# A third column pair by seven block products in the second layer's first FFN, with the key/value side work spread over fewer blocks

## The chip, the cores and the metric

The kernel runs on one core of a Trainium2 chip, as one launch. The metric is device time in microseconds (us), the median of several runs. TensorE is PE in the profile, its weight loads PEld, VectorE is DVE, ScalarE is ACT, GpSimd is POOL and SyncE is SP.

## The reference, cut to what matters

Two layers work on 256 tokens of width 1024, in float32. Each layer is a half step of SwiGLU, an attention, and a second half step of SwiGLU. After the first layer, keys and values for the second layer's attention are derived once.

```python
def _swiglu(x, w_in, w_out):
    a, b = jnp.split(x @ w_in, 2, axis=-1)
    return (jax.nn.silu(a) * b) @ w_out

for layer in range(DEPTH):
    h = h + 0.5 * _swiglu(_rmsnorm(h, ffn1_norm[layer]), ffn1_w_in[layer], ffn1_w_out[layer])
    hn = _rmsnorm(h, mix_norm[layer])
    ...
    h = h + 0.5 * _swiglu(_rmsnorm(h, ffn2_norm[layer]), ffn2_w_in[layer], ffn2_w_out[layer])
    if layer == N_A_LAYERS - 1:
        kvs = _nsa_shared_kv(h, kv_norm, nsa_w_kv, nsa_k_norm, cmp_pos_k, cmp_pos_v, ...)
```

`w_in` is 1024 x 5632 and `w_out` is 2816 x 1024. `_nsa_shared_kv` projects `h` to keys and values, compresses two of the six groups by a small hidden layer (`_compress`), normalizes and rotates the keys.

## The kernel before, in words

**Precision.** Every weight tile of 128 x 1024 (a *unit*) arrives by DMA as float32 and is split in two fp32r tiles: ScalarE writes the high part `wh` (L222), VectorE the rest `wl` (L226). Each product is then three matmuls (`mm3`, L290 to L292): high by high, high by low, low by high. The class `Weights` walks one long list of units in order: `pump` splits the next one, `take` hands it to TensorE, `done` gives its buffers back. There are six buffers each for `wh` and `wl`, and five for arriving tiles. An engine takes its instructions strictly in the order in which they were written to its queue; a scheduler makes that order before the run.

**Ordinary blocks.** The input projection of an FFN is cut into 11 blocks of 256 columns of `a` and the matching 256 of `b`. A block takes four units and 48 matmuls of 512 columns, in four pieces (`proj_block`): two units by the first 128 tokens, the same two by the other 128, then the other two units in the same way. `gate` (L648 to L659) makes silu(a)*b of a token half, and `gtrans` (L661 to L672) transposes a block's gates on TensorE (`gTp`) and splits them.

**Pairs.** Two neighbouring blocks can be done together by Strassen's scheme (Winograd's form): seven products p1 to p7 of block sums, in place of eight. A product is two units and 12 matmuls. The sums of the activations are made once (`sums_of_h`), the sums of weights per pair. In the other three FFNs the weight sums come partly by DMA; in this one, `f11` (second layer, first FFN), VectorE makes them: L228 (`keep` plus the joined tile), L234 (`keep` plus a raw tile), L221 (a raw tile plus a held one), two of 128 x 1024 for each of the four kinds of step, eight in a pair. A pair also has two sums on product banks (`x`, L759).

**The order of a pair** is a string in `FAST`. A digit is a product, `c` is an output chunk (`chunk`: one unit of `w_out`, 12 matmuls into the four `o` banks), `m` transposes one block's gates, `s` runs one piece of side work. `FAST["f11"]` has ordinary blocks 0 to 6, then the pairs (7, 8) and (9, 10), with eight chunks in each.

**Side work.** Beside the ordinary blocks of `f11` run 15 pieces of the key/value work (the list `side` at the end of `kv_phase`): compressed keys are transposed (`c_trans`, `xtp`), GpSimd adds positions (`c_blocks`, L1224), `c_split` splits the result, `c_hidden` 0 to 3 (two units of `cmp` each, 16 matmuls of 256 columns into the bank `hid`), `k_trans` 0 and 1 (`kTp`), `c_out` (transposes `hidT`), `c_out2` (`co`), `c_key` with `c_val_t` (`vcT`), and `c_key_t` (`kcT`). `hid` is finished by a copy on ScalarE (L1254), a sum on VectorE (L1255) and a silu on ScalarE (L1256) before `hidT`. In the loop over ordinary blocks, a piece of side work was run after pieces 1 and 3 of each block; the fifteenth by the `s` of pair (7, 8). `CMP_J = 4` placed the `cmp` units in the list of units.

Of the kernel before, what the change touches and what calls it, by code (L numbers as in the profile page):

```python
# [16 lines left out]
P = 128  # L17
# [2 lines left out]
FF = 2816  # L20
NB = FF // 256
J1 = 6
CMP_J = 4
LOW = 100


FAST = {"f10": (0,1,2,(3,"cccm1ctc5ct367xx24"),(5,"mc1mct5ct3c67xx24"),(7,"mc1mct5ct3c67xx24"),(9,"mc1mct5t36724")),
# [3 lines left out]


# [45 lines left out]
class Sum:  # L78


    def __init__(self, key, load=None, join=None, last=False):
        self.key, self.load, self.join, self.last = key, load, join, last
        self.more = ()


class Unit:


    def __init__(self, ap, key=None, of=None, hold=None, held=None):
        self.ap, self.key, self.of, self.hold, self.held = ap, key, of, hold, held  # L90
        self.more = ()


class Weights:


    def __init__(self, tc, pool, units, raws, bufs):
        self.tc, self.nc, self.pool, self.units = tc, tc.nc, pool, units
        self.raws, self.bufs = raws, bufs
        self.raw, self.hi, self.lo = {}, {}, {}  # L100
        self.on_pool = ()
        self.keep, self.kept, self.missed, self.waiting, self.held = None, {}, 0, [], {}
        self.limit, self.turn, self.pin = len(units), 0, False
        self.jobs, self.jobs_from = [], 0
        self.spans, self.extra = [], None
        self.nr = self.nl = self.ns = self.nt = self.nd = 0
# [94 lines left out]
    def pump(self, slack=1, low=LOW):  # L201

        u = self.ns
        if u >= (self.limit if slack else len(self.units)) or not self.room(u, slack):
            return False
        x = self.units[u]
        if self.keep is None and not isinstance(x, bass.AP) and x.key or self.apart(u) and self.extra is None:
            return False
        while self.nl <= u:
            self.load()  # L210
        nc = self.nc
        n = x.shape[-1] if isinstance(x, bass.AP) else 1024
        hi, lo = self.hi[u], self.lo[u] = self.pair_of(u)
        if not isinstance(x, Sum):
            raw = self.raw.pop(u)
        else:
            raw = self.kept.pop(x.key) if x.last else self.kept[x.key]
        prio = self.tc.cur_priority
        self.tc.cur_priority = prio + low
        if isinstance(x, Unit) and x.held:  # L220
            nc.vector.tensor_tensor(raw, raw, self.held.pop(x.held), op=OP.add)  # L221
        i = nc.scalar.activation(hi[:, 0:n], raw[:, 0:n], AF.Copy)  # L222
        if self.pin:
            self.tc.keep_in_program_order(i)
        e = nc.gpsimd if u in self.on_pool else nc.vector
        e.tensor_tensor(lo[:, 0:n], raw[:, 0:n], hi[:, 0:n].bitcast(F32), op=OP.subtract)  # L226
        if isinstance(x, Sum) and x.join is not None:
            nc.vector.tensor_tensor(raw, raw, self.raw.pop(u), op=OP.add)  # L228
        if isinstance(x, Unit) and x.hold:
            self.held[x.hold] = raw  # L230
        if isinstance(x, Unit) and x.key:
            y = self.kept[x.of or x.key]
            t = self.tile_of(x.key) if x.of else y
            nc.vector.tensor_tensor(t, y, raw, op=OP.add)  # L234
        for op in () if isinstance(x, bass.AP) else x.more:
            if self.keep is None:
                self.waiting.append(op)
            else:
                self.sum_op(*op)
        self.tc.cur_priority = prio  # L240
        self.ns += 1
        self.load()
        if self.jobs and u >= self.jobs_from:
            self.jobs.pop(0)()
        return True
# [13 lines left out]
def build(tc, ctx, a, out):  # L259
    nc = tc.nc  # L260
# [34 lines left out]
    units = []  # L295
# [54 lines left out]
    def fast(l):  # L350

        b = lambda j, k: [a[l[:2] + "i" + l[2]][4 * j + 2 * k + i] for i in range(2)]
        v, r = [], range(2)
        outs = [a[l[:2] + "o" + l[2]][i] for i in chunk_order(l)]
        pairs = [e[0] for e in FAST[l] if isinstance(e, tuple)]

        def also(d, op):
            if isinstance(v[d], bass.AP):
                v[d] = Unit(v[d])
            v[d].more += (op,)  # L360

        for e in FAST[l]:
            if not isinstance(e, tuple):
                v += b(e, 0) + b(e, 1)
                continue
            j, pat, *n = e
            z = pairs.index(j)
            b11, b21, b12, b22 = b(j, 0), b(j, 1), b(j + 1, 0), b(j + 1, 1)
            key = [(j, "t", i) for i in r]
            at = stored.get((l, j))  # L370
            third = lambda z, i: (pairs[z], 2, i)
            kept = lambda last=False: [Sum(key[i], last=last) for i in r]
            plus = [(third(z, i), b22[i], True) for i in r] if at is None else []
            own = l != "f11"
            ahead = []
            if own and z == 0 and at is None:
                for i in r:
                    also(i - 2, (third(0, i), b12[i], False))
            if own and z + 1 < len(pairs) and (l, pairs[z + 1]) not in stored:
                ahead = [(third(z + 1, i), b(pairs[z + 1] + 1, 0)[i], False) for i in r]  # L380
            for ch in pat:
                if at is not None and ch in "1536724":
                    x = {"1": b11, "3": b22, "2": b21, "5": at[0], "7": at[1], "6": at[2], "4": at[3]}[ch]
                    v += [Unit(x[i]) for i in r]
                elif ch == "1":
                    v += [Unit(b11[i], key=key[i], of=third(z, i)) if own else Sum(key[i], load=b11[i], join=b12[i])
                          for i in r]
                elif ch in "56":
                    v += kept()
                elif ch == "3":  # L390
                    v += [Unit(b22[i], key=key[i], hold=None if own else key[i]) for i in r]
                elif ch == "7":
                    v += [Sum(third(z, i), last=True) if own else Unit(b12[i], held=key[i]) for i in r]
                elif ch == "2":
                    v += [Unit(b21[i], key=key[i]) for i in r]
                elif ch == "4":
                    v += kept(True)
                elif ch == "c":
                    v += [Unit(outs.pop(0))]
                elif ch == "f":  # L400
                    v += b(n[0], 0)
                elif ch == "g":
                    v += b(n.pop(0), 1)
                elif ch in "tx":
                    also(-1, (plus if ch == "t" else ahead).pop(0))
            assert not ahead and (not own or not plus)
        if l == "f11":
            return v + outs
        v += outs
        units.extend(v)  # L410
# [22 lines left out]
    add("sbo"), wide("f20")  # L433
    add("kv")
    f1i1 = fast("f11")
    units.extend(f1i1[:4 * CMP_J])
    cw = len(units)
    for i in range(4):
        units.extend(a["cmp"][j] for j in range(2 * i, 2 * i + 2))
        units.extend(f1i1[4 * CMP_J + 2 * i:4 * CMP_J + 2 * i + 2])  # L440
    units.extend(f1i1[4 * CMP_J + 8:])
    add("nsi0"), add("nsi1")
    nso = len(units)
    add("nso"), wide("f21")
    W = Weights(tc, wp, units, raws=5, bufs=6)
    spans[0] = (2, spans[0][1])
    W.spans = spans
    W.on_pool = ()


    h = rp.tile([P, 2, D], F32, name="h")
# [178 lines left out]
    def ffn(l, hT, rs, post, targets, side=(), pool=None, start=None, room=new_room):  # L630
        side = list(side)

        j0 = [isinstance(j, tuple) for j in FAST[l]].index(True)
        with ExitStack() as es:
# [210 lines left out]
            if start:  # L845
                twin()
            else:
                for j in range(j0):
                    o = accs("a") if j or l == "f11" else [zbank("a") for _ in range(2)]
                    for i, f in enumerate(proj_block(512, hT, j == 0, post, o)):  # L850
                        f()
                        if j and i == 1:
                            gtrans(j - 1)
                        if i % 2 == 1 and side:
                            side.pop(0)()
                        if i == 2:
                            gate(j, 0, o)
                    gate(j, 1, o)
# [24 lines left out]
            n = 2 * NB - 4  # L883
# [765 lines left out]
    with tc.tile_pool(name="kvp", bufs=1, side="right") as kp:  # L1649
# [5 lines left out]
        side = kv_phase(n3, rs, post, st)  # L1655
# [113 lines left out]
```

## Time and profile before

| | |
|---|---|
| median of 3 runs | 995.5 us (995.35 to 997.32) |
| the profiled execution | 994.79 us, of which the span is 993.0 us |
| granted TensorE clock | 1.00 |
| busy: PE, DVE, ACT, POOL | 983.4, 873.7, 698.2, 114.9 us |
| `f11`, from its first block's matmul to the start of the attention's projection | 515.87 to 710.26 us of the span |

Times in the rows are counted from the start of the span. A row of the timeline gives the start and the duration of an instruction and, in brackets, how long its engine stood idle before it and what ended that. Durations of matmuls overlap, so that the distance of starts is what a matmul costs. A busy TensorE can hold a bottleneck or only follow one, so that the stretches matter more than the shares.

### The profile page before, as it was taken

To read this page: it belongs to the slowest core of one execution; us is meant where nothing else is said; L and a number is where in the kernel's file an instruction comes from. 1 tells how busy PE (TensorE), PEld (TensorE's weight loads), DVE (VectorE), ACT (ScalarE), POOL (GpSimd) and SP (SyncE) were. 2 spreads that over 40 slices of the span, in tenths; PEclk is the share of its full clock that TensorE was granted. 3 is DMA by queue.
4 is the path that set the end of the run, shared out by engine and by line. 5 is a ranking of instruction groups with operands and counts; after the bars stand their busy time and mean duration, and the time that the engine had idled before them with its cause. 6 is when DMAs were issued, how large, how long until landed. Compare 5 with 4: busy or idle time off the path is not lost.

```text
span 993.0 us, 14093 instructions
## 1 busy us (share of the span) xinstructions
PE 983.4 (99%) x4961; PEld 817.1 (82%) x4961; DVE 873.7 (88%) x1149; ACT 698.2 (70%) x1099; POOL 114.9 (12%) x184
## 2 busy tenths in 40 slices
PE   9999999999999999999999999999999999999998
PEld 6787888898988788878888887888897888788887
DVE  7899999878879999999778698898668879999996
ACT  6776767577868767777565775666669958767763
POOL 0000000010000000000217101000056500000000
PEclk9999999999999999999999999999999999999999
DMA  9988774599846978775996789667330186977761
GB/s 332 355 244 254 222 211 144 176 303 292 247 151 225 332 230 250 235 208 171 273 318 206 252 278 245 235 207 219 114 121 1 45 311 228 310 231 216 250 170 43
DMA packets 65479, 219.89 MB, mean 221 GB/s; under 512 B 7168, under 2 KB 9216, under 8 KB 65408
## 3 DMA queue, kind: packets, MB, share of 16 engines
q1 hardware_dynamic: 58336, 197.86, 58.3%
q0 software_dynamic: 6784, 20.97, 12.1%
q8 instruction: 39, 0.64, 0.3%
q14 instruction: 32, 0.26, 0.1%
q10 hardware_dynamic: 288, 0.16, 0.1%
HBM read 212.67 MB, written 13.63 MB: 228 GB/s over the span
## 4 chain that ended last, share of the span: by engine, by line
PE 69%; issue 13%; DVE 8%; DMA 4%; ACT 3%; POOL 2%; SPq 0%; ACTq 0%; DVEq 0%; POOLq 0%
PE o L291 6%; PE o L292 6%; PE o L290 6%; PE c L290 5%; PE c L292 5%; PE c L291 5%; DVE wl L226 4%; PE a L290 3%; PE a L292 2%; PE a L291 2%; PE cu L290 2%; PE cu L292 2%; PE cu L291 2%; DMA keep<-in_f1i 2%; PE qk L948 2%
## 5 line engine op out<-in xcount | busy, mean ns | idle before, releaser
L226 DVE TENSOR_TENSOR wl<-wraw,wh 128x1024 fp32r<-128x1024 f32 (+2 forms) x316 | 377.1, 1210 | 37.4 <-ACT wh L222 35.7
L222 ACT ACTIVATE wh<-wraw 128x1024 fp32r<-128x1024 f32 (+2 forms) x316 | 322.6, 1044 | 71.1 <-PE o L292 23.8
L222 ACT ACTIVATE wh<-keep 128x1024 fp32r<-128x1024 f32 x112 | 116.6, 1056 | 68.5 <-DVE keep L234 48.8
L226 DVE TENSOR_TENSOR wl<-keep,wh 128x1024 fp32r<-128x1024 f32 x112 | 132.7, 1216 | 6.2 <-ACT wh L222 5.9
L234 DVE TENSOR_TENSOR keep<-keep,wraw 128x1024 f32<-128x1024 f32 x80 | 97.2, 1215 | 1.6 <-DMA wraw<-in_f1i 1.6
L291 PE MATMUL o<-wl,gTh0f 128*128 128x512 f32 x192 | 75.0, 391 | 0.3 <-DVE wl L226 0.3
L290 PE MATMUL o<-wh,gTh0f 128*128 128x512 f32 x192 | 74.8, 397 | 0.0
L292 PE MATMUL o<-wh,gTl0f 128*128 128x512 f32 x192 | 74.6, 391 | 0.0
L290 PE MATMUL o<-wh,gTh1f 128*128 128x512 f32 (+1 forms) x160 | 62.5, 399 | 0.0
L291 PE MATMUL o<-wl,gTh1f 128*128 128x512 f32 (+1 forms) x160 | 62.1, 388 | 0.0
L292 PE MATMUL o<-wh,gTl1f 128*128 128x512 f32 (+1 forms) x160 | 61.3, 388 | 0.0
L290 PE MATMUL a<-wh,hT_f 128*128 128x512 f32 x144 | 57.5, 399 | 0.0
L290 PE MATMUL c<-wh,hT_f 128*128 128x512 f32 x144 | 56.6, 393 | 0.0
L292 PE MATMUL a<-wh,hT_f 128*128 128x512 f32 x144 | 56.3, 391 | 0.0
L291 PE MATMUL a<-wl,hT_f 128*128 128x512 f32 x144 | 56.3, 391 | 0.0
L291 PE MATMUL c<-wl,hT_f 128*128 128x512 f32 x144 | 56.2, 390 | 0.0
L292 PE MATMUL c<-wh,hT_f 128*128 128x512 f32 x144 | 56.2, 390 | 0.0
L290 PE MATMUL cu<-wh,sums 128*128 128x512 f32 x112 | 44.6, 398 | 1.0 <-ACT cp L754 1.0
L290 PE MATMUL c<-wh,sums 128*128 128x512 f32 x112 | 44.3, 396 | 0.1
L292 PE MATMUL cu<-wh,sums 128*128 128x512 f32 x112 | 43.8, 391 | 0.0
L292 PE MATMUL c<-wh,sums 128*128 128x512 f32 x112 | 43.7, 390 | 0.0
L291 PE MATMUL c<-wl,sums 128*128 128x512 f32 x112 | 43.6, 389 | 0.0
(346 smaller groups left out, 2365.0 us busy)
## 6 DMA issues: line engine op xcount, KB each, us to landing
wraw<-in_f1i SPq DMA_DIRECT2D x76, 512.0 KB, 4.8
wraw<-in_f2i SPq DMA_DIRECT2D x68, 512.0 KB, 5.0
wraw<-in_f1o SPq DMA_DIRECT2D x44, 512.0 KB, 4.7
wraw<-in_f2o SPq DMA_DIRECT2D x44, 512.0 KB, 4.8
wraw<-in_sbqk SPq DMA_DIRECT2D x16, 512.0 KB, 4.6
wraw<-sf SPq DMA_DIRECT2D x16, 512.0 KB, 4.5
keep<-in_f2i SPq DMA_DIRECT2D x16, 512.0 KB, 4.5
keep<-in_f2i POOLq DMA_DIRECT2D x16, 512.0 KB, 8.8
```

The source lines that it names most:

```text
L222: i = nc.scalar.activation(hi[:, 0:n], raw[:, 0:n], AF.Copy)
L226: e.tensor_tensor(lo[:, 0:n], raw[:, 0:n], hi[:, 0:n].bitcast(F32), op=OP.subtract)
L234: nc.vector.tensor_tensor(t, y, raw, op=OP.add)
L290: nc.tensor.matmul(o, xh, wh, start=start, stop=False, skip_group_check=True)
L291: nc.tensor.matmul(o, xh, wl, start=False, stop=False, skip_group_check=True)
L292: nc.tensor.matmul(o, xl, wh, start=False, stop=stop, skip_group_check=True)
L948: nc.tensor.matmul(oi, wh[:, c], xh, start=k == 0 and q == 0, stop=False, skip_group_check=True)
```

## The change

Blocks 5 and 6 of `f11`, two ordinary blocks, become a third pair. The 16 output chunks beside the pairs are spread anew over three pairs (5, 5 and 6). The side work now runs after pieces 1, 2 and 3 of each of the five ordinary blocks that are left, so that its 15 pieces end with them and no `s` is left in a pattern. The `cmp` units move to the places at which the pieces want them.

```diff
-CMP_J = 4
+CMP_AT = (12, 12, 14, 16)
+SIDES = (1, 2, 3)
...
-        "f11": (0,1,2,3,4,5,6,(7,"cs1ccm5cc3cc67c24"),(9,"cm1cmc5cc3cc67c24")),
+        "f11": (0,1,2,3,4,(5,"1ccm5c3c67c24"),(7,"mc1cm5c3c67c24"),(9,"mc1cmc5c3c67c24")),
...
-    units.extend(f1i1[:4 * CMP_J])
-    cw = len(units)
-    for i in range(4):
-        units.extend(a["cmp"][j] for j in range(2 * i, 2 * i + 2))
-        units.extend(f1i1[4 * CMP_J + 2 * i:4 * CMP_J + 2 * i + 2])
-    units.extend(f1i1[4 * CMP_J + 8:])
+    for i, n in enumerate(CMP_AT + (len(f1i1),)):
+        units.extend(f1i1[CMP_AT[i - 1] if i else 0:n])
+        if i < 4:
+            units.extend(a["cmp"][j] for j in range(2 * i, 2 * i + 2))
...
                         if j and i == 1:
                             gtrans(j - 1)
-                        if i % 2 == 1 and side:
+                        if i in SIDES and side:
                             side.pop(0)()
```

A new letter `p` for a pattern, which would move a low part to GpSimd (`slow`), replaces the unused `on_pool`; no pattern has it, so it changes no instruction.

How the instructions move is seen best around `hidT`. These are rows of TensorE's order before, at that place; `a0` and `a1` are the banks of an ordinary block for the two token halves, and the number behind `wh` or `wl` is the unit's place in the list.

```order
L666 MATMUL gTp_5944<-cst_96,g_5903 128x128
L291 MATMUL a1_5907<-wl260_5888,hT_f11_5092 128x512
L292 MATMUL a1_5907<-wh260_5887,hT_f11_5092 128x512
L290 MATMUL a1_5907<-wh261_5926,hT_f11_5092 128x512
L291 MATMUL a1_5907<-wl261_5927,hT_f11_5092 128x512
L292 MATMUL a1_5907<-wh261_5926,hT_f11_5092 128x512
L290 MATMUL a1_5907<-wh261_5926,hT_f11_5092 128x512
L291 MATMUL a1_5907<-wl261_5927,hT_f11_5092 128x512
L292 MATMUL a1_5907<-wh261_5926,hT_f11_5092 128x512
L1262 MATMUL hidT_6028<-cst_96,hid_5981 128x64 x4
```

And these are the rows of TensorE's order after the change; the last row of `hid` stands 16 matmuls ahead of `hidT`.

```order
L290 MATMUL a1_5692<-wh251_5711,hT_f11_5092 128x512
L291 MATMUL a1_5692<-wl251_5712,hT_f11_5092 128x512
L292 MATMUL a1_5692<-wh251_5711,hT_f11_5092 128x512
L290 MATMUL a0_5861<-wh254_5758,hT_f11_5092 128x512
L291 MATMUL a0_5861<-wl254_5759,hT_f11_5092 128x512
L292 MATMUL a0_5861<-wh254_5758,hT_f11_5092 128x512
L290 MATMUL a0_5861<-wh254_5758,hT_f11_5092 128x512
L1264 MATMUL hidT_5850<-cst_96,hid_5817 128x64 x4
L291 MATMUL a0_5861<-wl254_5759,hT_f11_5092 128x512
```

Before, 24 matmuls and a `gTp` stood between `hid` and `hidT`; now 16 matmuls do, four of them of the fifth block. On ScalarE the chain of `hid` stood like this before (L1254 is its copy, L1256 its silu):

```order
L222 ACTIVATE wh264_5973<-wraw264_5930 128x1024
L222 ACTIVATE wh265_6007<-wraw265_5942 128x1024
L1254 ACTIVATE hid_5981<-hid_5710 64x512
L653 ACTIVATE sil_5997<-a0_5906,rstd_4865 128x256
L1256 ACTIVATE hid_5981<-hid_5981 64x512
```

Since the change (copy L1256, silu L1258), two splits stand between the copy and the silu:

```order
L222 ACTIVATE wh256_5809<-wraw256_5748 128x1024
L1256 ACTIVATE hid_5817<-hid_5592 64x512
L222 ACTIVATE wh257_5831<-wraw257_5762 128x1024
L222 ACTIVATE wh258_5843<-keep_5797 128x1024
L1258 ACTIVATE hid_5817<-hid_5817 64x512
```

A second place is the first `kTp` bank, which the next `gTp` takes over. VectorE's order after the change has both readers of that bank (`kDl`) between splits:

```order
L226 TENSOR_TENSOR wl248_5645<-wraw248_5605,wh248_5644 128x1024
L660 TENSOR_TENSOR g_5688<-a1_5533,sil_5687 128x256
L226 TENSOR_TENSOR wl249_5659<-wraw249_5619,wh249_5658 128x1024
L1195 TENSOR_TENSOR kDl_4946<-kTp_5678,kDh_4945 64x2x256
L226 TENSOR_TENSOR wl250_5673<-wraw250_5636,wh250_5672 128x1024
L226 TENSOR_TENSOR wl251_5712<-wraw251_5648,wh251_5711 128x1024
L1195 TENSOR_TENSOR kDl_4946<-kTp_5678,kDh_4945 64x2x256
```

On TensorE 16 matmuls of `hid`, the four transposes `kTp` and 24 matmuls of the fourth block lie between the end of the third block and that `gTp`; before, the next `gTp` started 18.7 us after the first `kTp` (573.39 and 592.08 us).

More of the change, by code (lines that the diff above doesn't have):

```diff
@@ L82, in __init__ @@
         self.key, self.load, self.join, self.last = key, load, join, last
-        self.more = ()
+        self.more, self.slow = (), False
 class Unit:
@@ L90, in __init__ @@
         self.ap, self.key, self.of, self.hold, self.held = ap, key, of, hold, held
-        self.more = ()
+        self.more, self.slow = (), False
 class Weights:
@@ L100, in __init__ @@
         self.raw, self.hi, self.lo = {}, {}, {}
-        self.on_pool = ()
         self.keep, self.kept, self.missed, self.waiting, self.held = None, {}, 0, [], {}
@@ L224, in pump @@
             self.tc.keep_in_program_order(i)
-        e = nc.gpsimd if u in self.on_pool else nc.vector
+        e = nc.gpsimd if not isinstance(x, bass.AP) and x.slow else nc.vector
         e.tensor_tensor(lo[:, 0:n], raw[:, 0:n], hi[:, 0:n].bitcast(F32), op=OP.subtract)
@@ L403, in fast @@
                     v += b(n.pop(0), 1)
+                elif ch in "pP":
+                    for d in range(-1 - (ch == "P"), 0):
+                        if isinstance(v[d], bass.AP):
+                            v[d] = Unit(v[d])
+                        v[d].slow = True
                 elif ch in "tx":
@@ L447, in build @@
     W.spans = spans
-    W.on_pool = ()
     h = rp.tile([P, 2, D], F32, name="h")
```

1 row of the table FAST is left out of this document.

## The prediction

> **What bounds the kernel now.** I read the page first, then stretches of `f11`, then its timeline. Of the page, span and busy shares:
>
> ```profile
> span 993.0 us, 14093 instructions
> PE 983.4 (99%) x4961; PEld 817.1 (82%) x4961; DVE 873.7 (88%) x1149; ACT 698.2 (70%) x1099; POOL 114.9 (12%) x184
> ```
>
> TensorE is busy nearly always. Whether it is the limit in `f11` shows in the stretches: ordinary blocks with side work, first pair, second pair, last chunks.
>
> ```profile
> core 0: us, PE busy (x) PEld busy (x) DVE busy (x) ACT busy (x) POOL busy (x), PEclk, DMA share, GB/s
> 515.87:607.72 91.85, 91.78 (x465) 76.29 (x463) 73.29 (x94) 58.82 (x80) 24.98 (x33) 1.00 0.82 256
> 607.72:649.80 42.08, 42.08 (x188) 34.15 (x187) 37.16 (x41) 27.91 (x37) 1.96 (x3) 1.00 0.71 217
> 649.80:691.66 41.86, 41.86 (x190) 34.50 (x189) 40.03 (x41) 28.35 (x33) 0.00 (x0) 1.00 0.67 215
> 691.66:700.00 8.34, 8.34 (x42) 6.96 (x41) 4.16 (x6) 3.46 (x5) 0.00 (x0) 1.00 0.58 177
> ```
>
> TensorE loses 0.07 us in 184. So `f11` costs what its matmuls cost, and any wait that appears on TensorE is added to the time. The second pair already fills VectorE to 40.03 of 41.86 us. What a matmul costs is seen in TensorE's timeline, from the first row of one chunk to the first row of the product behind it, 12 matmuls later:
>
> ```profile
> 630.66 0.39 PE L290 MATMUL o<-wh,gTh0f 128*128 128x512 f32 x1
> 633.38 0.39 PE L290 MATMUL cu<-wh,hT_xb 128*128 128x512 f32 x1
> ```
>
> 12 matmuls take 2.72 us, one 0.227 us, without a gap.
>
> **The change part by part.** *Matmuls.* Two blocks were 96 matmuls, a pair is 7 x 12 = 84. The gain is 12 x 0.227 = 2.7 us, all on the path. No other TensorE work is added: gates, their transposes, chunks and side work keep their number.
>
> *VectorE.* From the grouped lines of both pairs:
>
> ```profile
> L226 DVE TENSOR_TENSOR wl<-wraw,wh 128x1024 fp32r<-128x1024 f32 x31 | 37.1, 1217 | 1.9 <-ACT wh L222 1.7
> L234 DVE TENSOR_TENSOR keep<-keep,wraw 128x1024 f32<-128x1024 f32 x8 | 9.7, 1215 | 1.6 <-DMA wraw<-in_f1i 1.6
> ```
>
> A pair adds 14 - 8 = 6 splits and 8 sums, 14 x 1.2 = 17 us of VectorE, and 6 splits and a few copies on ScalarE, which has room (28 of 42 us). VectorE doesn't: the two pairs with eight chunks held 37.16 + 40.03 = 77.2 us, 38.6 each, in 42 us of TensorE. A pair with five chunks loses three: 38.6 - 3 x 1.2 = 35.0 us against 42 - 3 x 2.72 = 33.8 us. With six chunks it is 36.2 against 36.5. Over the three pairs VectorE is asked for 106.2 us in 104.1, 2.1 too much. What carries it is its lead. Two splits of VectorE before the second pair, and the matmuls that first use their low parts:
>
> ```profile
> 639.79 1.23 DVE L226 TENSOR_TENSOR wl<-keep,wh 128x1024 fp32r<-128x1024 f32 x1 [0.35 <-ACT wh L222]
> 645.94 0.39 PE L291 MATMUL c<-wl,hT_f 128*128 128x512 f32 x1
> ...
> 647.71 1.21 DVE L226 TENSOR_TENSOR wl<-keep,wh 128x1024 fp32r<-128x1024 f32 x1
> 651.85 0.39 PE L291 MATMUL c<-wl,hT_f 128*128 128x512 f32 x1
> ```
>
> A lead of 4.9 us shrinks to 2.9 where one pair follows another. There the next pair's `keep` tile is fetched only when the last split of the pair before has read it, and ScalarE waits for it:
>
> ```profile
> 643.37 1.06 ACT L222 ACTIVATE wh<-keep 128x1024 fp32r<-128x1024 f32 x1 [1.20 <-DMA keep<-in_f1i]
> ```
>
> The change has two such joints. The first starts from the lead of before and ends at 2.9. The five-chunk pair between takes 1.2 from the lead of 4.9, and the second joint 2.0 more, so about 1.7 is left, with further copies in between that VectorE waits for. I take 0.5 us of waiting there; the bounds are 0 and 3 (a rival, below).
>
> *Side work, first place: `gTp` behind `kTp`.* The bank of the first `kTp` goes to the `gTp` of the fourth block. ScalarE and VectorE read it as here (timeline of before):
>
> ```profile
> 573.16 2.35 DVE L226 TENSOR_TENSOR wl<-wraw,wh 128x1024 fp32r<-128x1024 f32 x2
> 575.43 0.68 DVE L1193 TENSOR_TENSOR kDl<-kTp,kDh 64x512 fp32r<-64x512 f32 x1
> 576.03 0.67 DVE L712 TENSOR_TENSOR hT_xb<-hg,hT_xb 128x512 fp32r<-128x512 f32 x1
> 576.64 0.42 DVE L658 TENSOR_TENSOR g<-a,sil 128x256 f32<-128x256 f32 x1
> ...
> 573.39 0.63 PE L1187 MATMUL kTp<-cst,kva 128*128 128x128 f32 x4
> 573.77 0.47 PE L290 MATMUL a<-wh,hT_f 128*128 128x512 f32 x1
> ...
> 587.79 0.28 PE L1248 MATMUL hid<-wl,hT_xb 128*128 128x256 f32 x1
> 588.27 0.28 PE L1248 MATMUL hid<-wl,hT_xb 128*128 128x256 f32 x1
> ```
>
> A chained split costs 1.14 us (2.35 for two), a `kDl` 0.61, a gate 0.35, a `hid` matmul 0.12, four transposes 0.38. Count from the end of the third block. TensorE reaches `gTp` after 16 x 0.12 + 0.38 + 24 x 0.227 and a little at each change of bank: 7.9 us. VectorE gets its next split 1.35 us in (the buffer, then ScalarE's split), and in its new order stand four splits, a gate, two `kDl` and one split more ahead of the bank's release: 1.35 + 5 x 1.14 + 0.35 + 2 x 0.61 = 8.6. TensorE waits 0.7 us (bounds 0 and 1.5).
>
> *Second place: `hidT`.* TensorE's last rows that read a buffer, then ScalarE and VectorE in the chain of `hid`, before:
>
> ```profile
> 584.89 0.39 PE L292 MATMUL a<-wh,hT_f 128*128 128x512 f32 x1
> ...
> 585.37 1.06 ACT L222 ACTIVATE wh<-wraw 128x1024 fp32r<-128x1024 f32 x1 [0.34 <-PE a L292]
> 586.73 2.96 ACT L222 ACTIVATE wh<-wraw 128x1024 fp32r<-128x1024 f32 x3 [0.30 <-PE a L292]
> 589.59 0.57 ACT L1254 ACTIVATE hid<-hid 64x512 f32<-64x512 f32 x1
> 592.06 0.63 ACT L1256 ACTIVATE hid<-hid 64x512 f32<-64x512 f32 x1 [0.25 <-DVE hid L1255]
> ...
> 591.35 0.68 DVE L1255 TENSOR_TENSOR hid<-hid 64x512 f32<-64x512 f32 x1
> ```
>
> A split starts 0.1 us after the last matmul that reads its buffer (584.89 + 0.39, then 585.37). Count from the end of the last `c_hidden`. After the change ScalarE's order is split 256, copy, split 257, split 258, silu. Split 257 needs the buffer of unit 251, last read by the 12th matmul: 0.1 + 11 x 0.227 + 0.39 + 0.1 = 3.1. Two splits (0.98 each, from 2.96 for three) and the silu (0.63) end at 5.7. TensorE is at `hidT` after 16 matmuls, at 3.7, and waits 1.9 us, with the fifth block behind it. Bounds: 0, since copy, sum and silu alone need only 0.57 + 0.68 + 0.63 = 1.9, and 3 if split 258's `keep` is late. Before, `hidT` came 6.1 us in, behind a silu that was done.
>
> *Third place: `kcT`.* The chain from the compressed keys, before:
>
> ```profile
> 605.59 0.20 DVE L1283 TENSOR_REDUCE css<-csq 64x1 f32<-64x64 f32 x1
> 605.82 0.15 DVE L1284 TENSOR_SCALAR css<-css 64x1 f32<-64x1 f32 x1
> 606.64 0.28 DVE L1287 SCALAR_TENSOR_TENSOR kd<-co,css,vec 64x64 f32<-64x64 f32 x1 [0.67 <-POOL css L1285]
> 607.85 0.19 DVE L1290 COPY kd<-kd 64x64 f32<-64x64 f32 x1 [0.94 <-POOL kd L1329]
> ```
>
> From `css` to the copy's end are 2.45 us. VectorE's new order puts a copy, a `keep` sum, a `gTl`, a split and a part of the values ahead, about 4.1 us from the end of `co`: 6.5 with the chain. TensorE needs 24 matmuls and `vcT`, 6.0 us. It waits 0.5 (bounds 0 and 1.5). Before, `kcT` stood in the pairs, long after.
>
> *GpSimd.* `c_blocks` and the rotation follow each other more closely; a row has their price:
>
> ```profile
> L1224 POOL TENSOR_TENSOR kvb<-kvb,vec x16: 441/454/1445, 525.3 to 555.0; 128x120 f32<-128x120 f32 x16
> ```
>
> The second eight start near 540 and, mostly at the price of 0.45, end near 545, before ScalarE wants them near 547. I take nothing.
>
> *Queues.* SyncE has two more loads of 512 KB per pair; the stretches ran at 0.67 to 0.71 of the DMA engines, so nothing. The eight `kDh`/`kDl` copies move ahead of two loads that are needed 5 us later or more; nothing.
>
> *Sum.* -2.7 + 0.7 + 1.9 + 0.5 + 0.5 = +0.9 us. The profiled execution, 994.8 us (span 993.0 and 1.8 around it), becomes 995.7; the median before lies 0.7 higher, so I forecast **996.4 us**. 2 us, 0.2%, is about what a measurement of this kernel tells from no change.
>
> **The rivals.** *All waits hidden: 992.8 us.* For it: `f11` had no wait before, and the chains alone are short (1.9 us for `hid`). Against: the order is fixed, and the buffer of unit 251 comes late whatever happens. It gives 995.5 - 2.7 and decides if ScalarE reaches the silu within 3.7 us. [...] 0.2.
>
> *VectorE becomes the limit in the pairs: 999 us.* For it: 40.03 of 41.86 us, and idle time that no lead removes, about 2 us a pair (1.7 <-ACT wh, 1.6 <-DMA in the two groups). Then 106.2 + 6 = 112.2 us stand against 104.1 and a lead of 4.9, so that 3.2 us are missing in place of my 0.5: 996.4 + 2.7. It decides when the lead at the second joint is gone. Against: half of the idle time was VectorE having nothing to do. 0.18.
>
> *GpSimd is locked out: 1001 us.* If the second eight `c_blocks` cost 1.445 us each, they end at 540 + 11.6 = 551.6, 4.7 us after ScalarE wants them, and the first `hid` products wait: 996.4 + 4.7. Against: 0.45 is the median of the 16. [...] 0.07.
>
> **How the numbers follow.** Forecast 0.55, rivals 0.2, 0.18, 0.07. Faster by over 0.2% is the first rival, 0.2; slower the other two, 0.25; within 0.2% the forecast, 0.55. The range leaves out half of the first rival and the last: 993.0 to 1000.0.
>
> **What would show it.** In the profile after, TensorE should idle about 2 us before `hidT` with ScalarE's silu as releaser, and under 1 us before the fourth block's `gTp` (released by `kDl`) and before `kcT`; the pairs should run at 0.227 us a matmul. Wrong would be: no idle TensorE before `hidT`, or repeated waits for `wl` in the third pair.

## The result, and the profile after

The changed kernel takes **1003.2 us** (median of 4 runs, 1000.99 to 1003.66); the kernel before takes 995.5 us (median of 4 runs, 995.35 to 997.32). The ratio is 1.0067, with a 95% interval from 1.005 to 1.0083: slower by 0.5 to 0.8%, and above the range of the prediction. The profiled execution took 1003.12 us, of which the span is 1001.3.

Line numbers after the change are two higher than before it. First the busy shares on the page of the changed kernel:

```profile
PE 984.8 (98%) x4949; PEld 816.4 (82%) x4949; DVE 890.7 (89%) x1165; ACT 704.5 (70%) x1109; POOL 116.9 (12%) x184
```

The twelve matmuls are gone (4949 in place of 4961) and VectorE does 16 instructions more: the 14 that the prediction counted and two sums on product banks. The span grew by 8.3 us all the same. The stretches of `f11` show where: ordinary blocks, then the three pairs. The first pair counts from the end of the ordinary blocks, and the columns are those of the prediction's stretches.

```profile
514.84:587.85 73.01, 69.94 (x362) 57.36 (x360) 62.91 (x84) 48.55 (x69) 27.10 (x33) 1.00 0.82 249
587.85:624.42 36.57, 36.57 (x165) 30.10 (x165) 31.58 (x35) 23.67 (x30) 1.85 (x2) 1.00 0.77 234
624.42:664.69 40.27, 37.49 (x154) 29.52 (x152) 34.93 (x36) 23.35 (x31) 0.00 (x0) 0.92 0.62 196
664.69:701.40 36.71, 36.50 (x162) 29.54 (x161) 36.58 (x37) 26.57 (x33) 0.00 (x0) 1.00 0.63 204
```

Before, TensorE was idle for 0.07 us in `f11`. Now it is idle for 3.07 us beside the ordinary blocks and for 2.78 us in the second pair, and in the second pair alone the granted clock is 0.92. In the third pair VectorE is busy for 36.58 of 36.71 us. What TensorE waited for, in `f11` (the columns are named in the first line):

```profile
engine line waited for: us in total, times, longest us
PE xtp L1211 <- DVE kva L1208: 1.9, 1, 1.9
PE cu L290 <- ACT cp L756: 1.3, 1, 1.3
PE o L291 <- DVE wl L226: 1.0, 1, 1.0
PE gTp L668 <- DVE g L660: 0.6, 1, 0.6
...
PE kTp L1189 <- DVE gTl0f L674: 0.4, 1, 0.4
...
PE kcT L1296 <- DVE kd L1292: 0.2, 1, 0.2
```

There is no `hidT` in this list, and `xtp` at its top is a place that the prediction didn't walk through. Waits of over 0.5 us cost about 0.2 us more than their rows say: by the distances of starts 0.9 us for the row of 0.6 (`gTp`) and 2.05 us for that of 1.9 (`xtp`).

**The two waits near the start.** TensorE's timeline at the second `gTp` row and the second `xtp`, then VectorE's at the same time:

```profile
533.05 0.55 PE L668 MATMUL gTp<-cst,g 128*128 128x128 f32 x3 [0.65 <-DVE g L660]
...
541.41 0.63 PE L1211 MATMUL xtp<-cst,kva 128*128 128x128 f32 x4 [1.85 <-DVE kva L1208]
```

```profile
529.58 1.00 DVE L1208 COPY kva<-kva 128x256 f32<-128x256 f32 x2
530.50 0.90 DVE L717 TENSOR_TENSOR hg<-hg 128x512 f32<-128x512 f32 x1
...
532.58 0.41 DVE L660 TENSOR_TENSOR g<-a,sil 128x256 f32<-128x256 f32 x1
...
538.86 1.21 DVE L1232 TENSOR_TENSOR hT_xb<-kvb,hT_xb 128x1024 fp32r<-128x1024 f32 x1
539.99 0.41 DVE L660 TENSOR_TENSOR g<-a,sil 128x256 f32<-128x256 f32 x1
540.33 0.94 DVE L1208 COPY kva<-kva 128x256 f32<-128x256 f32 x2
```

No row has a bracket: VectorE's queue is full here. Before, the gate of block 0 stood ahead of these copies:

```profile
532.29 0.41 DVE L658 TENSOR_TENSOR g<-a,sil 128x256 f32<-128x256 f32 x1
532.62 0.72 DVE L1206 COPY kva<-kva 128x256 f32<-128x256 f32 x2
```

The copies (L1208) from which `xtp` transposes now come a piece earlier, and so does `c_split` (L1232), which began at 547.75 us before. The gate of block 0 now stands behind two copies as well, and the copies for the second `xtp` behind `c_split` and a gate. TensorE loses 0.9 us at 532 and 2.05 us at 541.

**The second pair.** VectorE's timeline in the first pair (first row) and at the first joint, ScalarE's at the joint, and then TensorE's 25 us later:

```profile
606.49 1.22 DVE L234 TENSOR_TENSOR keep<-keep,wraw 128x1024 f32<-128x1024 f32 x1 [1.85 <-DMA wraw<-in_f1i]
...
621.28 1.23 DVE L226 TENSOR_TENSOR wl<-keep,wh 128x1024 fp32r<-128x1024 f32 x1 [2.46 <-ACT wh L222]
```

```profile
620.18 1.06 ACT L222 ACTIVATE wh<-keep 128x1024 fp32r<-128x1024 f32 x1 [2.28 <-DMA keep<-in_f1i]
```

```profile
644.91 0.50 PE L290 MATMUL o<-wh,gTh0f 128*128 128x512 f32 x1 [0.51 <-ACT wh L222]
646.37 0.50 PE L291 MATMUL o<-wl,gTh0f 128*128 128x512 f32 x1 [0.95 <-DVE wl L226]
...
648.66 0.79 PE L290 MATMUL cu<-wh,hT_xb 128*128 128x512 f32 x1 [1.32 <-ACT cp L756]
...
650.11 0.63 PE L290 MATMUL cu<-wh,hT_xb 128*128 128x512 f32 x1
650.54 0.63 PE L291 MATMUL cu<-wl,hT_xb 128*128 128x512 f32 x1
```

VectorE stood idle for 1.85 and 2.46 us, although it had work to come: its next instruction wanted a tile that was late. At the joint that is a loop through VectorE itself: the load of the tile was issued at 615.15 us, when VectorE's split of 613.91 to 615.12 had read the buffer, and ScalarE could begin at 620.18. From 621.3 to 651.9 us VectorE then worked without a break of 0.15 us, and TensorE's three waits fall into that time. ScalarE's splits ahead of the first one began at 641.72, 0.1 us behind a sum of VectorE (L221); its copy `cp`, for the third, stood behind two splits that had waited 0.28 and 0.87 us for arriving tiles. So I take it that the idle time of the first pair is what is missing 25 us later.

I measured the lead (from the end of VectorE's split of a unit to the first matmul that reads it) along the pairs: 9.7 us at unit 260, in the first pair; 3.3 at unit 276; 0.8 at unit 279, behind the first joint; 0.05 at units 291 and 298. From the first joint on it comes back to 1 us or less again and again (0.8 at unit 286, 1.0 at unit 315), with up to 9 us between, the most where TensorE stood or ran slowly. The last rows show something else: after three waits, matmuls start 0.43 us apart in place of 0.227, twelve in a row, and are back to 0.23 near 654.4.

By place, TensorE lost against its own pitch: 2.9 us at the two early waits, 0.5 at `kTp`, 0.5 about `kcT`, 6.0 in the second pair (2.5 of it in the slow matmuls) and 0.6 in the third. That is 10.5; less 2.7 for the twelve matmuls it makes 7.8, of the 8.1 us by which `f11` grew.

### The profile page after: what moved, and what is told of

The parts are those of the page before. It is cut to its first block, busy times and chain, and to the rows that moved or that the text cites. A ratio compares the mean times of both kernels' runs of the same rounds, so it can differ in the third digit from the quotient of the medians.

```text
span 1001.3 us, 14093 instructions
## 1 busy us (share of the span) xinstructions
PE 984.8 (98%) x4949; PEld 816.4 (82%) x4949; DVE 890.7 (89%) x1165; ACT 704.5 (70%) x1109; POOL 116.9 (12%) x184
## 3 DMA queue, kind: packets, MB, share of 16 engines
q1 hardware_dynamic: 58624, 198.90, 58.3%
## 4 chain that ended last, share of the span: by engine, by line
PE 66%; issue 15%; DVE 9%; DMA 4%; ACT 3%; POOL 2%; SPq 0%; ACTq 0%; DVEq 0%; POOLq 0%
PE o L291 7%; PE o L292 6%; PE o L290 6%; PE c L290 5%; PE c L292 5%; PE c L291 5%; DVE wl L226 4%; PE cu L290 2%; PE cu L291 2%; PE cu L292 2%; PE qk L950 2%; PE qk L951 1%; PE qk L952 1%; PE gTp L668 1%; DMA wraw<-in_f1i 1%
## 5 line engine op out<-in xcount | busy, mean ns | idle before, releaser
L222 ACT ACTIVATE wh<-keep 128x1024 fp32r<-128x1024 f32 x120 | 125.2, 1056 | 68.6 <-DVE keep L234 52.2
L226 DVE TENSOR_TENSOR wl<-keep,wh 128x1024 fp32r<-128x1024 f32 x120 | 142.2, 1217 | 5.3 <-ACT wh L222 4.9
L234 DVE TENSOR_TENSOR keep<-keep,wraw 128x1024 f32<-128x1024 f32 x84 | 102.2, 1216 | 1.8 <-DMA wraw<-in_f1i 1.8
L290 PE MATMUL c<-wh,hT_f 128*128 128x512 f32 x156 | 61.3, 393 | 0.0
L291 PE MATMUL c<-wl,hT_f 128*128 128x512 f32 x156 | 60.9, 391 | 0.2 <-DVE wl L226 0.2
L292 PE MATMUL c<-wh,hT_f 128*128 128x512 f32 x156 | 60.8, 390 | 0.0
L290 PE MATMUL a<-wh,hT_f 128*128 128x512 f32 x112 | 45.1, 402 | 0.0
L291 PE MATMUL a<-wl,hT_f 128*128 128x512 f32 x112 | 43.8, 391 | 0.0
L292 PE MATMUL a<-wh,hT_f 128*128 128x512 f32 x112 | 43.8, 391 | 0.0
L291 PEld LDWEIGHTS o<-wl,gTh0f 128*128 128x128 f32 x192 | 36.2, 189 | 9.1 <-DVE wl L226 2.0
```

What stands on the lines that cost most here:

```text
L290: nc.tensor.matmul(o, xh, wh, start=start, stop=False, skip_group_check=True)
L291: nc.tensor.matmul(o, xh, wl, start=False, stop=False, skip_group_check=True)
L292: nc.tensor.matmul(o, xl, wh, start=False, stop=stop, skip_group_check=True)
```

## The experiments

`f11` is the time from the first `a` matmul of its first block to the last `o` matmul, in the profiled execution. The part of the program ahead of it is the same in all but the two kernels with sums from memory, and even so it began between 514.8 and 517.1 us there. So `f11` tells small differences better than a span. It is read from one execution of each kernel, though: in e5, e7, e8, e12 and e13 the slowest of its runs, in e4 the fastest.

| kernel | us, median (lowest to highest, runs) | before beside it | ratio, 95% interval | `f11`, us |
|---|---|---|---|---|
| before | 995.5 | | | 193.81 |
| the change | 1003.21 (1000.99 to 1003.66, 4) | 995.51 | 1.0067 [1.005, 1.0083] | 201.87 |
| e1 side work alone | 998.64 (997.31 to 1001.04, 7) | 995.28 | 1.004 [1.0027, 1.0053] | 198.90 |
| e2 pairs, side work late | 1000.99 (999.16 to 1005.06, 6) | 995.28 | 1.0063 [1.0044, 1.0082] | 198.59 |
| e3 half of the sums | 998.08 (997.5 to 999.6, 6) | 995.28 | 1.0028 [1.0014, 1.0042] | 195.63 |
| e4 ten low parts on GpSimd | 1016.83 (1011.41 to 1018.62, 4) | 995.28 | 1.0225 [1.0202, 1.0248] | 209.33 |
| e5 late, half of the sums | 997.39 (994.92 to 999.33, 10) | 996.63 | 1.0004 [0.9992, 1.0015] | 196.20 |
| e7 sums from memory | 1016.61 (1014.41 to 1018.57, 4) | 996.63 | 1.0205 [1.0184, 1.0225] | 197.63 |
| e8 the same, late | 1012.91 (1011.43 to 1013.42, 4) | 996.63 | 1.0166 [1.0151, 1.0181] | 194.75 |
| e9 six matmuls added | 1005.44 (1004.2 to 1006.46, 4) | 995.36 | 1.0102 [1.0088, 1.0116] | 201.53 |
| e10 chunks 4, 6, 6 | 1002.87 (1002.49 to 1005.17, 5) | 995.36 | 1.0081 [1.0067, 1.0094] | 201.30 |
| e11 late, chunks 4, 6, 6 | 997.16 (994.74 to 998.75, 11) | 995.36 | 1.0013 [1.0004, 1.0022] | 195.51 |
| e12 the same, two chunks first | 995.1 (993.3 to 996.37, 11) | 995.63 | 0.9989 [0.9981, 0.9998] | 193.98 |
| e13 the same, chunks 3, 6, 7 | 999.13 (995.56 to 1000.86, 12) | 995.63 | 1.0032 [1.0022, 1.0043] | 198.15 |

The theories: **A**, the side work, run three pieces to a block, makes VectorE late for `gTp` and `xtp` in the first blocks. **B**, VectorE with its late tiles sets the pace of the pairs from the first joint on. Rivals are named with each run.

**e1: the side work alone.** The two pairs of before, with the new placing of side work.

```diff
-        "f11": (0,1,2,3,4,(5,"1ccm5c3c67c24"),(7,"mc1cm5c3c67c24"),(9,"mc1cmc5c3c67c24")),
+        "f11": (0,1,2,3,4,5,6,(7,"cs1ccm5cc3cc67c24"),(9,"cm1cmc5cc3cc67c24")),
```

> The old two pairs and seven ordinary blocks, with the side work in three pieces per block, so that it ends with the fifth block. Theory A (the packed side work fills VectorE's queue in the first two blocks, and TensorE waits there for a gate and for the copies ahead of a transpose, 0.9 + 2.0 us): 998 to 999 us, with these two waits in the trace and none in the pairs. Theory B alone (all of the loss comes from VectorE in the five-chunk pairs): 995.5 us, as before.

All of TensorE's waits in `f11`:

```profile
PE kTp L1189 <- DVE gTl0f L674: 2.1, 1, 2.1
PE xtp L1211 <- DVE kva L1208: 1.9, 1, 1.9
PE gTp L668 <- DVE g L660: 0.6, 1, 0.6
```

`f11` is 5.1 us longer than before, with no wait in the pairs; the three places lose 0.87, 2.04 and 2.15 us, which is all of it. A holds: the side work alone makes the kernel slower, and none of the loss is at a place that the prediction priced.

**e2: the pairs with the side work late.** Two pieces per block in the first two blocks, as before, and more in the last; `cmp` units later.

```diff
-CMP_AT = (12, 12, 14, 16)
-SIDES = (1, 2, 3)
+CMP_AT = (14, 16, 16, 18)
+SIDES = ((1, 3), (1, 3), (1, 2, 3), (1, 2, 3), (0, 1, 2, 3))
...
-                        if i in SIDES and side:
+                        if l == "f11" and i in SIDES[j] and side:
```

The first pair's pattern begins with an `s` for the fifteenth piece.

> All three pairs as changed, but the first two blocks carry two pieces of side work each, as before; the third and fourth carry three, the fifth four, and the last piece stands in the first pair. Theory A: the waits of the first two blocks go, about 3 us less than the changed kernel, 1000 us; the wait in the second pair stays. Theory B alone: no change, 1003 us. A rival to both: the side work's chain now ends later and TensorE waits at hidT or kcT, 1003 us or more.

```profile
PE cu L290 <- ACT cp L756: 1.7, 1, 1.7
PE hidT L1264 <- ACT hid L1258: 1.1, 1, 1.1
...
PE kcT L1296 <- DVE vcBl L1313: 0.7, 1, 0.7
```

The early waits are gone. Of the 3.4 us that they and `kTp` had cost, 2 are lost again at the end of the side work, where `hidT` and `kcT` now do wait. ScalarE's timeline there, the last split and the silu behind it:

```profile
578.80 1.06 ACT L222 ACTIVATE wh<-wraw 128x1024 fp32r<-128x1024 f32 x1 [1.58 <-DMA wraw<-in_f1o]
579.77 0.61 ACT L1258 ACTIVATE hid<-hid 64x512 f32<-64x512 f32 x1
```

Splits stand between copy and silu, as forecast, but what this one waits for is an arriving tile, not a free buffer. The pairs still wait, for VectorE and for ScalarE behind it, so A is not the whole of it.

**e3: half of the sums.** L221 and L228 are left out, four of a pair's eight sums of weights, here and in e5, so that these two kernels compute something else.

```diff
-            nc.vector.tensor_tensor(raw, raw, self.held.pop(x.held), op=OP.add)
+            self.held.pop(x.held)
...
-            nc.vector.tensor_tensor(raw, raw, self.raw.pop(u), op=OP.add)
+            self.raw.pop(u)
```

> The changed kernel without four of the eight VectorE sums of each pair (the joined tile and the held tile are not added), 12 sums or 14 us of VectorE less over the three pairs. Theory B: the wait in the second pair and the slow clock behind it go, 5 to 6 us less, 997 to 998 us; the waits of the first two blocks stay. Rival C (the loads into the five arriving tiles are late, VectorE only waits for them): the second pair still waits, 1001 us or more. Theory A alone: 1003 us.

Twelve sums of 1.22 us are gone, 14.6 us of VectorE in the three pairs, while the number of loads, of splits and of matmuls stays. Of TensorE's waits in `f11` this is the only one in the pairs:

```profile
PE o L291 <- DVE wl L226: 0.7, 1, 0.7
```

`f11` falls by 6.2 us, and the early waits stay (1.8 us for `xtp`, 0.7 for `gTp`). B holds: what VectorE is asked for in the pairs made the waits there. The run doesn't part its two halves, though: a tile whose sum is left out also comes free earlier, and so does the load behind it.

**e4: low parts on GpSimd.** The letter `p` behind a chunk gives its low part to GpSimd, and `P` those of the two chunks ahead of it. That makes ten chunks, one more than the expectation says.

```diff
-        "f11": (0,1,2,3,4,(5,"1ccm5c3c67c24"),(7,"mc1cm5c3c67c24"),(9,"mc1cmc5c3c67c24")),
+        "f11": (0,1,2,3,4,(5,"1ccPm5cp3c67c24"),(7,"mcp1cpm5cp3cp67c24"),(9,"mcp1cpmcp5c3c67c24")),
```

> The changed kernel with the low parts of nine output chunks in the three pairs made by GpSimd, three per pair, so that VectorE has 10 us less to do. Theory B: the second pair stops waiting, 997 to 998 us. Rival D (GpSimd is slower per tile and locks VectorE out, so that nothing is won): 1003 us or more. Theory A alone: 1003 us.

GpSimd's group of splits (instructions; busy time and mean ns of one; idle time before), then two of them in its timeline and VectorE's timeline beside them:

```profile
L226 POOL TENSOR_TENSOR wl<-wraw,wh 128x1024 fp32r<-128x1024 f32 x10 | 29.9, 2994 | 78.7 <-ACT wh L222 75.0 <-PE gTp L668 3.6
```

```profile
634.30 6.68 POOL L226 TENSOR_TENSOR wl<-wraw,wh 128x1024 fp32r<-128x1024 f32 x2 [4.47 <-ACT wh L222]
```

```profile
635.30 3.43 DVE L234 TENSOR_TENSOR keep<-keep,wraw 128x1024 f32<-128x1024 f32 x1
638.65 3.42 DVE L226 TENSOR_TENSOR wl<-wraw,wh 128x1024 fp32r<-128x1024 f32 x1
```

Rival D holds, in that nothing is won. A split takes GpSimd 2994 ns in the mean, where VectorE's take 1218 in the change. Of VectorE's 81 splits and sums of weights between 570 and 712 us, six take 2.5 to 3.4 us, each of them begun while a GpSimd split ran; the other 75 take 1.23 us at most, as before. Together the six cost 12 us more than before, as much as the ten splits of which VectorE is relieved. TensorE waits 7.9 us at three places for low parts from VectorE, 3.4 at the longest. GpSimd's 12% is no room for this. The six were up to 2.2 us longer than in the change, beside GpSimd splits of at least 2.4 us. The run shows these times, not what makes them.

**e5: late side work and half of the sums.** The edits of e2 and e3 together.

> The side work placed late as in the run e2_side_late and four of the eight sums of each pair left out as in e3_half_the_sums. If the packed side work and VectorE in the pairs are all of the loss, what is left is the gain of 2.7 us less the late side work's own waits at hidT and kcT (1.3 and 0.7 us in e2): 994 to 995 us. If a third cause is at work (loads of the arriving tiles): 997 us or more, with waits in the pairs.

The two causes account for nearly all: 997.39 us, equal to before within its interval. It is above the 994 to 995 us expected, and in the range named for a third cause, but without that cause's waits: in the pairs there is one, of 0.7 us. The gain that the missing matmuls promised is not there, since `hidT` waits here too, for 1.9 us behind the same late tile as in e2. Behind that wait the matmuls again start 0.43 us apart for a while.

**e7 and e8: sums from memory.** Four sums of the pair (5, 6) are made in device memory by DMA during the first layer's second FFN, `f20`, as the kernel does for other pairs; e8 adds the late side work. (No run tests late loads directly, with a sixth arriving buffer for instance.)

```diff
+    store("f11", 0)
...
+    W.jobs, W.jobs_from = far_sums("f11", 5), W.ns + 4
```

> The changed kernel with the four weight sums of the pair (5, 6) made by DMA in device memory during the FFN before, so that VectorE has none of its eight sums and its seven products load finished tiles. Correct result. Theory B (VectorE's time in the pairs): the lead stays above 4 us into the second pair, its wait and the slow clock go, 997 to 998 us; the 2.9 us of the first two blocks stay. Rival C (it is the loads): seven products now load 14 tiles in place of 10, so the pairs wait as much or more, 1003 us.

> Sums of the pair (5, 6) made by DMA ahead, and the side work placed late: what both theories together would mend. 994 to 996 us; faster than before only if hidT and kcT wait for less than 2.7 us together. If either theory is wrong, 998 us or more.

Both are slower, by 20 and 16 us, and not in `f11`, which falls to 197.63 and 194.75 us. In `f20`, TensorE's longest wait in e7 and the stretch from 330 to 400 us around it:

```profile
PE c L290 <- ACT cp L757: 6.5, 1, 6.5
```

```profile
330.00:400.00 70.00, 60.31 (x249) 47.64 (x248) 53.73 (x56) 39.61 (x50) 6.29 (x7) 0.88 0.88 268
```

Before, the same 70 us held 314 matmuls in place of 249, at clock 1.00. So the sums by DMA relieve the pairs, as B says, and cost more than that where they are made, in a stretch that had no room either (VectorE 69.48 of 70 us before). Why `f20` loses as much was not followed further.

**e9: does the slow clock cost the time?** The first matmul of the second product in the second pair, which starts its bank anew, is issued six times more. That is 1.36 us of work ahead of the waits, with the same result. (`FILL` is 6, and that product alone passes 2 for `first`.)

```diff
+                            if l == "f11" and j == 7 and first == 2 and k == 0:
+                                for _ in range(FILL):
+                                    nc.tensor.matmul(o, x(0, k), wh[:, cc], start=True, stop=False, skip_group_check=True)
                             mm3(o, x(0, k), x(1, k), wh[:, cc], wl[:, cc], bool(first) and k == 0, k == 3)
```

> The change with the first matmul of the second product of the second pair (the one that starts its bank anew) issued six times more, which gives the same result: 6 x 0.227 = 1.4 us more work for TensorE, about 6 us ahead of its three waits of 0.5, 0.95 and 1.3 us there. Theory C (the half-pitch matmuls after the third wait come from TensorE standing still three times within 4 us; VectorE sets when the pair ends): the added matmuls take the place of waiting, the waits shrink by 1.4 us in all, the pitch stays at 0.227 us, and the time falls by the 2.5 us that the slow matmuls cost: 1000.7 us beside 995.5 of the kernel before. Rival (the slow stretch is not tied to the waits, or the waits don't shrink because their releasers follow TensorE): 1003.2 to 1004.6 us.

The same place of TensorE's timeline, and a later one in the third pair; then the stretch of the third pair:

```profile
648.59 0.50 PE L292 MATMUL o<-wl,gTh0f 128*128 128x512 f32 x1 [1.27 <-DVE wl L227]
649.16 0.40 PE L291 MATMUL o<-wh,gTh0f 128*128 128x512 f32 x1
649.39 0.39 PE L291 MATMUL cu<-wh,hT_xb 128*128 128x512 f32 x1
...
667.61 0.50 PE L292 MATMUL o<-wl,gTh1f 128*128 128x512 f32 x1 [1.54 <-DVE wl L227]
...
689.34 0.50 PE L291 MATMUL cu<-wh,hT_xb 128*128 128x512 f32 x1 [1.23 <-ACT cp L760]
```

```profile
665.67:703.00 37.33, 34.56 (x155) 28.00 (x154) 37.02 (x37) 25.25 (x32) 0.00 (x0) 1.00 0.65 212
```

With one wait in place of three the pitch stays at 0.23 us, as C has it. That the cost of the slow matmuls would then be saved was wrong. New waits of 1.5 and 1.2 us stand in the third pair, VectorE is busy for 37.02 of 37.33 us there, and `f11` is 201.53 us, 0.3 from the change's. In this execution, then, TensorE's added work and its clock made no difference to the length, as it should be if VectorE sets it. One execution of each kernel shows that, and the medians don't repeat it: e9's lies 2.2 us above the change's; 1.3 of the 1.7 us between the two profiled spans came ahead of `f11`, where the programs are alike, and what made it stays open.

**e10 and e11: the chunks 4, 6, 6**, with the side work early and late.

```diff
-(5,"1ccm5c3c67c24"),(7,"mc1cm5c3c67c24"),(9,"mc1cmc5c3c67c24")
+(5,"1cm5c3c67c24"),(7,"mc1cm5cc3c67c24"),(9,"mc1cmc5c3c67c24")
```

> The change with the 16 output chunks spread 4, 6, 6 over the three pairs in place of 5, 5, 6. Theory B (VectorE's lead runs out in the second pair, because a pair with five chunks asks VectorE for 35.0 us in 33.8 of TensorE): the first pair loses 2.7 us of a lead of 9.7 (33.8 against 31.1) in place of 1.2, the second loses nothing by its sums (36.2 against 36.5), the waits of the second pair shrink by 1 to 2 us and its slow matmuls (2.5 us) may go: 999.5 to 1002 us. Rival (the lead goes at the joint, by loads that come late, whatever the chunks): 1002.5 to 1005 us, with waits at the end of the first pair.

> The late side work of e2 together with the chunks spread 4, 6, 6. Theory A and B add: e2 gave 1001.0 beside 996.6, of which some 3.3 us were waits in the pairs and a slow stretch behind them; if the spread spares half of that, 998.5 to 999.5 beside 996, still slower than before, since waits for hidT and kcT (1.8 us) stay. Rival (loads at the joint set the lead): 1000.5 to 1002.

With the side work early, the spread alone does nothing that can be told from the change (201.30 us of `f11`). Its median of 1002.87 us is outside theory B's range and inside that of its rival, that the lead goes at the joint whatever the chunks. The early waits stay, and waits in all three pairs (2.5 us for `cp`, 1.9 for low parts) take the place of those in the second. With the side work late it gives 3.1 us of `f11` against e2, more than I expected. (The expectation sets e2's 1001.0 beside 996.6 us; the kernel before took 995.28 beside e2.) `hidT` doesn't wait, since no split that waits for a tile stands between copy and silu any more. What e11 still waits for is 1.7 us of high parts and 0.5 of low parts in the pairs.

**e12 and e13: two chunks ahead of the first product of a pair**, e13 with the spread 3, 6, 7.

```diff
-(5,"s1cm5c3c67c24"),(7,"mc1cm5cc3c67c24"),(9,"mc1cmc5c3c67c24")
+(5,"s1cm5c3c67c24"),(7,"mcc1m5cc3c67c24"),(9,"mcc1mc5c3c67c24")
```

> Late side work, chunks 4, 6, 6, and the second and third pair now begin with two output chunks in place of one (e11 with one chunk moved ahead of the first product in each). In e11 TensorE still lost 0.55 us at 604.2, 1.09 us at 619.1 and 1.5 us at 657.7 to 661, all but the first at the start of a pair. Theory B1 (at a joint the next pair's first tile is fetched late, and work that doesn't need it would cover it): the last two go, 2.6 us less, 994 to 995 beside 995.4. Rival B2 (VectorE has too much to do in all, so that a wait only moves): e11's 997 again, with the waits elsewhere.

> As e12, with the chunks spread 3, 6, 7. The first pair asks VectorE for 38.6 - 5 x 1.2 = 32.6 us in 42 - 5 x 2.72 = 28.4 and takes 4.2 us from a lead of some 9.7; the third gains one. Theory B1: waits appear in the first pair if the lead at its start is less than that and its idle time (about 2 us) together; 994.5 to 996. Rival B2: as much waiting as e12, only earlier: 996 to 997.5.

ScalarE at the first joint, e11 and then e12, each at the split of the next pair's first tile that waited longest:

```profile
619.85 1.06 ACT L222 ACTIVATE wh<-keep 128x1024 fp32r<-128x1024 f32 x1 [1.43 <-DMA keep<-in_f1i]
```

```profile
620.02 1.06 ACT L222 ACTIVATE wh<-keep 128x1024 fp32r<-128x1024 f32 x1 [1.07 <-DMA keep<-in_f1i]
```

The tile is late in both, but in e12 TensorE has a chunk more to do meanwhile, and the losses at the starts of pairs (1.1 and 1.5 us) shrink to 0.3 and 0. That supports late tiles at the joints as part of the cause. In part the wait only moves, as the rival has it: two for low parts, late in the second and third pair, are new. All of e12's waits in `f11`:

```profile
PE o L291 <- DVE wl L226: 1.1, 2, 0.6
PE hidT L1264 <- ACT hid L1258: 0.4, 1, 0.4
PE c L290 <- ACT wh L222: 0.4, 1, 0.4
```

With what the restarts cost, these take about the 2.7 us that the third pair saves, so `f11` is as long as before (193.98 and 193.81 us). e12 is the best version found, 995.1 us beside 995.6; half a microsecond is less than the 0.2% named in the prediction, and I take it for no change. e13 missed both expectations: with three chunks beside the first pair, TensorE loses some 4 us between 603 and 629 us. It seems that the lead at its start doesn't carry 4.2 us and VectorE's idle time together.

## Why the prediction was wrong, point by point

- **TensorE is the limit, and each wait is added.** Right ahead of the pairs, where e1's waits are all of its loss. In the pairs six matmuls more left e9's `f11` 0.3 us shorter, so that there TensorE's own work seems hidden behind VectorE's.
- **Matmuls, -2.7 us.** Right: 12 fewer, and the pitch is 0.227 us where nothing waits.
- **First failed step: the places.** I took each of three places at which the changed order looked tight and called the rest nothing. The first two blocks weren't among them. There the change moves copies and `c_split` ahead on VectorE, whose queue had no hole; it cost 2.9 us, and 5.1 in e1 together with a `kTp` wait that I hadn't priced either.
- **`gTp` behind `kTp`, 0.7.** It was 0. TensorE came to that `gTp` as counted, 7.8 us from the end of the third block (555.26 to 563.09 us). But VectorE's five splits began 0.15 us ahead of that end, not 1.35 behind it, and its second `kDl` was done at 562.5. The second `kTp` waited 0.4 us, for the reader of that `gTp`.
- **`hidT`, 1.9.** The largest term was 0. Split 257 didn't wait for the buffer of unit 251, whose last matmul began at 573.7 us. ScalarE's timeline of the change keeps the written order and has no idle time between the copy and the silu:

```profile
571.82 0.58 ACT L1256 ACTIVATE hid<-hid 64x512 f32<-64x512 f32 x1
572.30 1.05 ACT L222 ACTIVATE wh<-wraw 128x1024 fp32r<-128x1024 f32 x1
573.25 1.04 ACT L222 ACTIVATE wh<-keep 128x1024 fp32r<-128x1024 f32 x1
574.20 0.62 ACT L1258 ACTIVATE hid<-hid 64x512 f32<-64x512 f32 x1
```

  The silu ended 0.1 us ahead of `hidT`. I had taken the buffers to come free six units back, in the order of the list. The rows fit buffers that come free in the order of use: the last `cmp` units, 252 and 253, were read by 571.3 us, ahead of unit 251. In e2 and e5 the same chain did cost 1.1 and 1.9 us, through a late tile.
- **`kcT`, 0.5.** Its wait is 0.2 us, with some 0.3 more in the matmuls ahead of it; inside its bounds.
- **Second failed step: the pairs, 0.5 us at the second joint.** They lost 6.6 us, nearly all of it in the second pair, after the lead had gone at the first joint; my bounds were 0 and 3. I let the lead of 4.9 us go down by the arithmetic of sums (2.0 a joint, 1.2 a pair) and left VectorE's idle time out, though its rows stood in the same paragraph. The rival that VectorE becomes the limit had that term, 2 us a pair, and was right in kind; its "decides when the lead at the second joint is gone" was a pair too late, and its 3.2 us too few.
- **GpSimd.** Right: the second eight `c_blocks` took 2.75 and 2.31 us for four each, ended at 545.7 us, and `hid` didn't wait for them. The last rival took 1.445 us for each, the highest of its row; the change's own row has 1.437 as the highest and 0.564 as the median. What makes the highest, being locked out or anything else, no run shows.
- **Queues, nothing.** Wrong at the joints: the DMA engines' share (0.77 over the first pair) said nothing on a tile whose buffer comes free late. ScalarE waited 2.28 us for it.
- **The clock.** Not considered. The slow stretch cost 2.5 us at its place. Whether the change would be faster without it is not settled: e9, without it and with 1.4 us of work more, has an `f11` only 0.3 us shorter, while the one run of the change at clock 1.000 has a span of 999.2 us and the other three, at 0.997 and 0.998, have 1001.3 to 1001.9.

Not settled either is how the loss in the pairs divides between VectorE's sums and late tiles: e3 shows that both with fewer sums remove it, e12 that covering the joints removes some of it.

## What to carry to other kernels

When a change trades TensorE's work for VectorE's, count VectorE's idle time for late tiles with its busy time, and follow the lead to the end of the stretch, from the first joint on. When it moves small work closer together, walk through every place that the moved work passes, the early ones too, on the engine whose queue has no hole. A wait that is removed at one place is worth something only if the next engine's limit isn't right behind it: give the engine that waits more to do (e9) and see whether the time notices.

## What the runs showed of the hardware that I had not expected

After some short waits the matmuls came at about half the pace. In the change, four matmuls started between 644.9 and 648.6 us, beside waits of 0.51, 0.95 and 1.32 us, and the next twelve came 0.43 us apart; the granted clock is 0.50 from 647.60 to 654.42 us and 1.00 on both sides. In e7's `f20`, after waits of 1.11 and 1.28 us with one matmul between them, and in e5 after the single wait of 1.89 us for `hidT`, they came 0.43 us apart as well. The length of a wait alone doesn't decide it: after 1.27 and 1.54 us in e9 and after 1.85 us at `xtp` in the change they came 0.23 us apart, and e1's execution, with 2.1 us at `kTp`, has a mean granted clock of 1.000.

How long TensorE was busy just ahead doesn't decide it alone either. In the change it was busy for 2.28 of the 4 us before the granted clock fell (643.60 to 647.60 us), and for 2.15 of the 4 us around the wait at `xtp` (538 to 542 us), where the clock stayed at 1.00. No run shows what does decide it.
